# Shift and scale of x and context in two column halves with 2 KB rows, four channel chunks multiplied while the second half loads

## The chip, the cores and the metric

The kernel runs on one NeuronCore of one Trainium2 chip. The metric is the device time of one execution in microseconds; a run's time is compared as the median of several runs. The profile is of one execution of its own.

## The reference

One layer of a diffusion trunk on 512 latent tokens and 256 context tokens of width 1024. Both streams are normalised and modulated per channel by shift and scale, which are products of a conditioning vector with `w_mod`; three token mixers and a mixture of experts follow. What matters here is the start:

```python
mod_x = (sc @ w_mod[layer] + b_mod[layer]).reshape(-1, N_MOD, d)
mod_c = (scc @ w_mod[layer][:, :n_mod_c * d] + b_mod[layer][:n_mod_c * d]).reshape(1, n_mod_c, d)
hx = modulate(rms_norm(x, g_mix[layer]), mod_x[:, 0], mod_x[:, 1])
hc = modulate(rms_norm(ctx, g_mix[layer]), mod_c[:, 0], mod_c[:, 1])
px = split_columns(hx @ w_in[layer])
```

`sc` and `scc` are the silu of `c` and `c_ctx` (1024 each), `w_mod` is 1024 x 6144, and its first 2048 columns (shift, then scale) are the ones used at this place. `hx` and `hc` are multiplied with `w_in`.

## The kernel before

All is kept with channels on the 128 partitions, so the 1024 channels are eight chunks, k = 0 to 7. Products in f32 are made of two parts (a high half in fp32r and the rest as the low half): `hx` and `hc` are stored as such pairs, and every product of a weight chunk with a channel chunk is three matmuls (`quantum`, L310).

The stage this is about is `start` (L700). It computes the first two column units of `w_in`: the values (`wv`) and keys (`wk`) of the first retention head, for x (into PSUM tiles `px` and `om`, 512 columns) and for the context (into `oc`, 256 columns). Its steps per chunk k:

- `load_mod(k)` (L227) loads two tiles `wm` of 512 KB, shift and scale of chunk k: all 1024 rows of `w_mod`, 128 columns each, so rows of 512 bytes.
- `mod_rows` (L235) multiplies both tiles with the two conditioning vectors (`cpad`, 32 columns of which two are used). The eight row blocks go to four column groups of TensorE, two blocks each in turn; ScalarE copies the outcome (`rm`).
- `mod_cols` (L246) turns the outcome into columns with two small matmuls and adds the four groups; VectorE then makes `modT` and `am`.
- `turn_x`, `turn_c` (L255, L261) transpose the normalised x and context on TensorE, and `modulate` (L267) makes the high half on ScalarE and the low half on VectorE (`tf`, then the subtraction).
- `prod` (L721) makes the products of chunk k.

The order is written out by hand: from L732 to L812 `pinned` keeps the program order on every engine. The loop at L790 handles chunks 2 to 7; each round prepares chunk k + 1, makes the products of k, and makes `mod_rows` of k + 2. `pump.prime` and `pump.prime2` load and split weights of the later units, whose products (line 119) a scheduler may put between those of the stage. `tick` spreads small steps of the retention decays over the loop. `wm`, x and context share a pool of 14 tiles (L82). SyncE issues every load in order: four x tiles, wm of chunk 0, a `w_in` tile, wm of chunk 1, two context tiles, a `w_in` tile, and the other wm.

Of the kernel before, what the change touches and what calls it, by code (L numbers as in the profile page):

```python
# [8 lines left out]
F32 = mybir.dt.float32  # L9
# [40 lines left out]
def kernel(ctx, tc, x, c, cctx_x, c_ctx, w_mod, b_mod, g_mix, g_ffn, w_in, decay, ret_gn, w_ret,  # L50
# [20 lines left out]
    def dap(t, offset, ap):  # L71
        return bass.AP(tensor=t.tensor, offset=t.offset + offset, ap=ap)
# [15 lines left out]
    def h2(dtype=F32, name="h2", shape=(P, 512)):  # L88
        return H2p.tile(list(shape), dtype, name=name, tag="h2")
# [28 lines left out]
    def mm(o, lhsT, rhs, start, stop):  # L118
        PE.matmul(o, lhsT, rhs, start=start, stop=stop)  # L119
# [102 lines left out]
    def row_norm(i0, i1, half, E=V):  # L222
        for i in range(i0, i1):
            v = xs[i][:, half * 512:half * 512 + 512]
            E.tensor_scalar(v, v, rstd[:, i:i + 1], None, op0=OP.mult)

    def load_mod(k):  # L227
        ts = []
        for part in range(2):
            t = Tp.tile([P, KT, P], F32, name="wm", tag="t")  # L230
            SY.dma_start(t, dap(w_mod, part * D + k * P, [[NM, P], [P * NM, KT], [1, P]]))
            ts.append(t)
        return ts

    def mod_rows(wt):  # L235
        o = px()
        for part in range(2):
            for k2 in range(2):
                for g in range(4):
                    mm(o[32 * g:32 * g + 32, P * part:P * part + P], cpad[:, 4 * k2 + g, :],  # L240
                       wt[part][:, 4 * k2 + g, :], k2 == 0, k2 == 1)
        rm = h2(name="rm", shape=(P, 2 * P))
        A.activation(rm, o[:, 0:2 * P], AF.Copy)
        return rm

    def mod_cols(k, rm):  # L246
        o = px()
        for j in range(2):
            mm(o[:, 2 * j:2 * j + 2], rm[:, j * P:(j + 1) * P], sel2, True, True)
        b_ = colv[:, 16:32].rearrange("p (a k) -> p a k", a=2)[:, :, k:k + 1]  # L250
        V.tensor_tensor(modT[:, :, k, :], o[:, 0:4].rearrange("p (a n) -> p a n", a=2), b_.to_broadcast([P, 2, 2]),
                        op=OP.add)
        V.tensor_scalar(am[:, k, :], modT[:, 1, k, :], 1.0, colv[:, 32 + k:33 + k], op0=OP.add, op1=OP.mult)

    def turn_x(k):  # L255
        o = pa()
# [442 lines left out]

    def start():  # L700
        us = [r0[0], r0[2]]
        wm = [load_mod(0)]
        raw = [us[0].load()]
        wm.append(load_mod(1))
        for i in range(2):
            xs.append(Tp.tile([P, D], F32, name="xs", tag="t"))
            SY.dma_start(xs[4 + i], dap(cctx_x, i * P * D, [[D, P], [1, D]]))
        raw.append(us[1].load())
        wm.append(load_mod(2))
        wm.append(load_mod(3))  # L710

        def halves(raw, nm, E):
            r = []
            for b in range(2):
                hi, lo = [h2(F32R, name=nm, shape=(P, 4, P)) for _ in range(2)]
                A.activation(hi, raw[:, 4 * b:4 * b + 4, :], AF.Copy)
                E.tensor_tensor(lo, raw[:, 4 * b:4 * b + 4, :], f32(hi), op=OP.subtract)
                r.append((hi, lo))
            return r

        def prod(i, k, x=True, c=True):  # L721
            w = wsp[i][k // 4]
            us[i].quantum(k % 4, w, om[i][0] if x else None, om[i][1] if c else None, k=k)

        def mod_x(k, o):
            modulate(HX(k), HX(k, 1), o, k, 0)

        def mod_c(k, o):
            modulate(HC(k), HC(k, 1), o, k, 1)

        om = [(px(), OC()[:, :CTX]), (pa("om"), pa("oc")[:, :CTX])]
        pinned[0] = True  # L732
        for i in (0, 2):
            row_stat(i, i + 2)
            row_norm(i, i + 2, 0)
        ox, oc, rm = {}, {}, {}
        wsp = []

        dg = decays()

        def tick(n=2):
            for _ in range(n):
                next(dg, None)

        def rows_of(k):
            rm[k] = mod_rows(wm[k])
            if k < 4:
                wm.append(load_mod(k + 4))

        rows_of(0)  # L750
        ox[0] = turn_x(0)
        if HV == 0:
            wsp.append(halves(raw[0], "wv", V))
        mod_cols(0, rm[0])
        if HV == 1:
            wsp.append(halves(raw[0], "wv", V))
        mod_x(0, ox[0])
        ox[1] = turn_x(1)
        if HV == 2:
            wsp.append(halves(raw[0], "wv", V))  # L760
        rows_of(1)
        mod_cols(1, rm[1])
        prod(0, 0, c=False)
        mod_x(1, ox[1])
        wsp.append(halves(raw[1], "wk", G))
        row_stat(4, 6)
        prod(0, 1, c=False)
        row_norm(4, 6, 0)
        rows_of(2)
        prod(1, 0, c=False)  # L770
        mod_cols(2, rm[2])
        ox[2] = turn_x(2)
        prod(1, 1, c=False)
        oc[0] = turn_c(0)
        mod_c(0, oc[0])
        mod_x(2, ox[2])
        oc[1] = turn_c(1)
        mod_c(1, oc[1])
        rows_of(3)
        for i in range(2):  # L780
            prod(i, 0, x=False)
        oc[2] = turn_c(2)
        mod_c(2, oc[2])
        for i in range(2):
            prod(i, 1, x=False)
        ox[3] = turn_x(3)
        row_norm(0, 6, 1)
        rope_table(0)
        pump.prime()
        for k in range(2, KT):  # L790
            tick(T0)
            if k < 7:
                mod_cols(k + 1, rm[k + 1])
                tick(T1)
                mod_x(k + 1, ox[k + 1])
                tick(T2)
            for i in range(2):
                prod(i, k, c=False)
            if k < 7:
                oc[k + 1] = turn_c(k + 1)  # L800
                mod_c(k + 1, oc[k + 1])
                tick(T3)
            if k < 6:
                rows_of(k + 2)
            for i in range(2):
                prod(i, k, x=False)
            if k < 6:
                ox[k + 2] = turn_x(k + 2)
            if k == 5:
                pump.prime2()  # L810
        tick(99)
        pinned[0] = False  # L812
        ph0.close()
        pools["k3"] = ph1.enter_context(tc.tile_pool(name="k3p", bufs=11))
        pools["s5"] = ph1.enter_context(tc.tile_pool(name="s5p", bufs=8))
        for u, o in zip(us, om):
            u.done(*o)
# [906 lines left out]
```

## Time and profile before

| what | value |
|---|---|
| median of 3 runs | 1224.18 us (1221.31 to 1225.31) |
| the profiled execution | 1222.83 us |
| its span, first to last instruction | 1221.1 us |
| TensorE matmuls busy (PE) | 1156.3 us (95%) |
| TensorE weight loads (PEld) | 720.6 us (59%) |
| VectorE (DVE) | 618.3 us (51%) |
| ScalarE (ACT) | 402.9 us (33%) |
| GpSimd (POOL) | 87.7 us (7%) |
| mean DMA rate | 234 GB/s over 285.57 MB |

Times in rows are microseconds from the start of the span. PE is TensorE, and a matmul of f32 operands shows as two instructions. A busy engine is not the same as an engine at its peak: matmuls are pipelined, so of a row of equal matmuls the distance between starts is the price, not the duration of one. "Idle before <- X" says what ended an engine's wait.

### The profile page before, as it was taken

The page shows a single profiled execution, that of the slowest core. Times are in us where ns is not written, and L with a number is a line of the kernel's source. Part 1 is how long each engine was busy: PE and PEld are TensorE (multiplying, and loading weights), DVE is VectorE, ACT ScalarE, POOL GpSimd, SP SyncE. Part 2 cuts the span into 40 slices and gives each one's busy share as a digit, 9 for nine tenths or more (in the row PEclk, how much of TensorE's full clock was granted, in tenths as well). Part 3 has the DMA queues.
Part 4 walks back from the last instruction along what each step waited for, and adds up shares of the span by engine and source line. Part 5 has one row for each costly group of instructions (what it writes and reads, how often), then busy time and mean ns, then how long its engine had stood idle before and what let it go on. Part 6 is the DMA issues. An engine that isn't in the chain of part 4 may idle for free.

```text
span 1221.1 us, 15830 instructions
## 1 busy us (share of the span) xinstructions
PE 1156.3 (95%) x5869; PEld 720.6 (59%) x5869; DVE 618.3 (51%) x1383; ACT 402.9 (33%) x777; POOL 87.7 (7%) x149
## 2 busy tenths in 40 slices
PE   4999999899999999999999969999999999999995
PEld 2788888777668887788888854333333323233322
DVE  3787666788867764577646362233332222222213
ACT  4553334666645553333332222122111111111112
POOL 2011111100041120000000000000000000000001
PEclk9999999999999999999999979999999999999998
DMA  9822112211012115987638548999999999999994
GB/s 272 232 75 70 52 52 89 57 38 34 12 52 61 42 54 198 285 268 248 199 95 300 194 161 298 409 409 409 409 409 409 409 409 409 409 409 408 409 409 188
DMA packets 159978, 285.57 MB, mean 234 GB/s; under 512 B 10838, under 2 KB 100250, under 8 KB 159900
## 3 DMA queue, kind: packets, MB, share of 16 engines
q1 hardware_dynamic: 158172, 278.27, 62.7%
q0 software_dynamic: 1152, 4.19, 0.9%
q10 hardware_dynamic: 576, 2.10, 0.4%
q8 instruction: 46, 0.75, 0.3%
q14 instruction: 32, 0.26, 0.1%
HBM read 280.33 MB, written 4.19 MB: 233 GB/s over the span
## 4 chain that ended last, share of the span: by engine, by line
PE 61%; DMA 25%; DVE 8%; ACT 2%; issue 1%; SPq 1%; POOL 1%; DVEq 0%; POOLq 0%; ACTq 0%
PE px L119 26%; DMA rg<-in_w_exp_up_dram 16%; PE pa L67 10%; PE px L67 8%; DMA rg<-in_w_exp_down_dram 7%; PE pa L119 7%; PE PV L119 3%; PE oc L119 3%; DVE ws L295 1%; PE pa L1041 1%; PE pa L955 1%; PE oy L119 1%; DMA rw<-in_w_in_dram 1%; DMA wm<-in_w_mod_dram 1%; DVE rt L445 1%
## 5 line engine op out<-in xcount | busy, mean ns | idle before, releaser
L67 PE MATMUL pa<-rg,xe 128*64 128x512 f32 x1024 | 263.3, 607 | 7.1 <-DMA rg<-in_w_exp_up_dram 4.8
L67 PEld LDWEIGHTS pa<-rg,xe 128*64 128x64 f32 x1024 | 72.5, 137 | 154.8 <-issue 108.2
L67 PE MATMUL px<-rg,hid 128*64 128x512 f32 x512 | 120.3, 601 | 10.7 <-DMA rg<-in_w_exp_down_dram 9.9
L295 DVE TENSOR_TENSOR ws<-rw,ws 128x1024 fp32r<-128x1024 f32 x55 | 67.7, 1232 | 56.1 <-PE px L119 34.7
L67 PEld LDWEIGHTS px<-rg,hid 128*64 128x64 f32 x512 | 32.8, 136 | 90.2 <-issue 48.2
L119 PE MATMUL px<-hx0h,ws 128*128 128x512 f32 x224 | 83.3, 401 | 0.0
L119 PE MATMUL px<-hx3h,ws 128*128 128x512 f32 x224 | 83.3, 398 | 0.0
L119 PE MATMUL px<-hx1h,ws 128*128 128x512 f32 x224 | 82.6, 398 | 0.0
L119 PE MATMUL px<-hx2h,ws 128*128 128x512 f32 x224 | 82.2, 395 | 0.0
L67 DVE SCALAR_TENSOR_TENSOR tt<-px,gcol,m 128x512 f32<-128x512 f32 x16 | 12.0, 751 | 127.6 <-PE px L67 127.6
L67 ACT ACTIVATE yy<-tt 64x512 fp32r<-64x512 f32 x32 | 20.1, 628 | 144.6 <-DVE tt L67 144.2
L67 DVE TENSOR_TENSOR acc<-px,acc 128x512 f32<-128x512 f32 x58 | 37.5, 687 | 59.9 <-PE px L67 59.9
L119 PE MATMUL px<-yh,ws 128*128 128x512 f32 x192 | 62.3, 390 | 0.6 <-ACT mod L1165 0.6
L294 ACT ACTIVATE ws<-rw 128x1024 fp32r<-128x1024 f32 x55 | 57.8, 1052 | 5.6 <-DMA rw<-in_w_in_dram 5.1
L911 ACT ACTIVATE Sx<-Sx,nm 128x512 f32<-128x512 f32 (+1 forms) x64 | 47.9, 748 | 34.4 <-DVE nm L947 19.0
L1160 DVE SCALAR_TENSOR_TENSOR mac<-mw,cpad,mac 128x1024 f32<-128x1024 f32 x30 | 38.5, 1282 | 17.9 <-DMA mw<-in_w_mod_dram 15.6
L119 PEld LDWEIGHTS px<-hx3h,ws 128*128 128x128 f32 x224 | 42.1, 189 | 7.9 <-issue 1.1
L119 PEld LDWEIGHTS px<-hx0h,ws 128*128 128x128 f32 x224 | 42.2, 189 | 7.6 <-issue 0.7
L119 PEld LDWEIGHTS px<-hx1h,ws 128*128 128x128 f32 x224 | 42.3, 189 | 7.2
L119 PEld LDWEIGHTS px<-hx2h,ws 128*128 128x128 f32 x224 | 42.4, 189 | 6.9
L67 ACT ACTIVATE gu<-pa 128x512 f32<-128x512 f32 x16 | 9.5, 596 | 110.0 <-PE pa L67 110.0
L67 DVE TENSOR_SCALAR xe<-px,af,sf 128x128 f32<-128x128 f32 (+1 forms) x36 | 14.0, 403 | 62.1 <-ACT xe L67 43.3
(422 smaller groups left out, 2169.6 us busy)
## 6 DMA issues: line engine op xcount, KB each, us to landing
rg<-in_w_exp_gate_dram SPq DMA_DIRECT2D x128, 512.0 KB, 10.2
rg<-in_w_exp_up_dram SPq DMA_DIRECT2D x128, 512.0 KB, 10.2
rg<-in_w_exp_down_dram SPq DMA_DIRECT2D x128, 512.0 KB, 10.2
rw<-in_w_in_dram SPq DMA_DIRECT2D x58, 512.0 KB, 4.0
mw<-in_w_mod_dram SPq DMA_DIRECT2D x32, 512.0 KB, 5.2
wm<-in_w_mod_dram SPq DMA_DIRECT2D x16, 512.0 KB, 7.7
rw<-in_w_out_dram SPq DMA_DIRECT2D x8, 512.0 KB, 3.6
xs<-in_x_dram SPq DMA_DIRECT2D x4, 512.0 KB, 4.1
```

The lines of the kernel that those rows point to most:

```text
L67: return (lambda *a_, **k_: tc.keep_in_program_order(f(*a_, **k_))) if pinned[0] else f
L119: PE.matmul(o, lhsT, rhs, start=start, stop=stop)
L294: A.activation(hi, raw, AF.Copy)
L295: V.tensor_tensor(lo[:, :NV], raw[:, :NV], f32(hi[:, :NV]), op=OP.subtract)
L445: V.tensor_copy(t2[b:b + q], o[c:c + q])
L911: A.activation(Sx[:, :n], Sx[:, :n], AF.Exp, scale=-1.0, bias=nm, accum_out=l[:, 0:1])
L955: PE.transpose(o[:, j * P:(j + 1) * P], SXs[b, j][:, ti * P:(ti + 1) * P], ident)
L1041: PE.transpose(o[:, b * P:(b + 1) * P], SXs[a, b][:, ti * P:(ti + 1) * P], ident)
L1160: V.scalar_tensor_tensor(macs[w], tiles[i], cpad[:, k, 0:1], macs[w], op0=OP.mult, op1=OP.add)
```

## The change

The first 2048 columns of `w_mod` are loaded and multiplied in two halves: half 0 has shift and scale of chunks 0 to 3, half 1 those of chunks 4 to 7. A tile is two row blocks by 512 columns, so its rows are 2 KB. `load_mod(half, kp)` loads two such tiles (shift, scale), and `mod_rows` makes four matmuls of 512 columns per pair `kp`, into two PSUM tiles that collect the four pairs of a half. `mod_cols` runs once per half: two copies, eight small matmuls, and three VectorE instructions for four chunks. All of half 0 is loaded and multiplied ahead of the first product. In a loop over k = 0 to 3 the products of chunk k stand beside `mod_rows` of pair k of half 1; then `mod_cols` of half 1 and a loop over k = 4 to 7. The context products of both units share the PSUM tile `oc`. The normalising of the second halves of x and context moves into rounds 0 and 1.

```diff
-    def load_mod(k):
+    def load_mod(half, kp):
...
         for part in range(2):
-            t = Tp.tile([P, KT, P], F32, name="wm", tag="t")
-            SY.dma_start(t, dap(w_mod, part * D + k * P, [[NM, P], [P * NM, KT], [1, P]]))
+            t = Tp.tile([P, 2, 512], F32, name="wm", tag="t")
+            SY.dma_start(t, dap(w_mod, 2 * kp * P * NM + part * D + half * 512, [[NM, P], [P * NM, 2], [1, 512]]))
             ts.append(t)
...
-    def mod_rows(wt):
-        o = px()
+    def mod_rows(mo, kp, ts):
         for part in range(2):
-            for k2 in range(2):
-                for g in range(4):
-                    mm(o[32 * g:32 * g + 32, P * part:P * part + P], cpad[:, 4 * k2 + g, :],
-                       wt[part][:, 4 * k2 + g, :], k2 == 0, k2 == 1)
...
+            for i in range(2):
+                k = 2 * kp + i
+                g = k % 4
+                mm(mo[part][32 * g:32 * g + 32, :], cpad[:, k, :], ts[part][:, i, :], k < 4, k >= 4)
...
+    def mod_cols(half, mo):
+
+        o = pa("mc")
+        for part in range(2):
+            rm = h2(name="rm")
+            if part:
+                V.tensor_copy(rm, mo[part])
+            else:
+                A.activation(rm, mo[part], AF.Copy)
+            for j in range(4):
+                c_ = 8 * part + 2 * j
+                mm(o[:, c_:c_ + 2], rm[:, j * P:(j + 1) * P], sel2, True, True)
...
+        raw, wm = [us[0].load()], {}
+        for kp in range(4):
+            wm[0, kp] = load_mod(0, kp)
...
+        wsp = [halves(raw[0], "wv", V)]
+        ox, oc = {}, {}
+        mo = [px(), px()]
+        for kp in range(4):
+            mod_rows(mo, kp, wm[0, kp])
+            wm[1, kp] = load_mod(1, kp)
         ox[0] = turn_x(0)
...
+        mod_cols(0, mo)
+        row_stat(4, 6)
         mod_x(0, ox[0])
         ox[1] = turn_x(1)
...
         row_norm(4, 6, 0)
...
+        mo = [px(), px()]
+        for k in range(4):
+            prod(0, k, c=False)
+            if k == 0:
+                wsp.append(halves(raw[1], "wk", G))
+            oc[k] = turn_c(k)
+            mod_c(k, oc[k])
+            if k < 3:
+                mod_x(k + 1, ox[k + 1])
+                if k < 2:
+                    ox[k + 2] = turn_x(k + 2)
+            prod(1, k, c=False)
+            mod_rows(mo, k, wm[1, k])
+            for i in range(2):
+                prod(i, k, x=False)
+            if k == 0:
+                row_norm(0, 4, 1)
+            if k == 1:
+                row_norm(4, 6, 1)
+            tick(6)
         rope_table(0)
         pump.prime()
...
+        ox[4] = turn_x(4)
+        mod_cols(1, mo)
+        mod_x(4, ox[4])
+        ox[5] = turn_x(5)
+        oc[4] = turn_c(4)
+        mod_c(4, oc[4])
+        for k in range(4, KT):
             if k < 7:
...
                 mod_x(k + 1, ox[k + 1])
...
             for i in range(2):
                 prod(i, k, c=False)
```

The order of the loads on SyncE's queue, before, from the last x tile on (`xs` are x and context tiles, `rw` tiles of `w_in`):

```order
L148 DMA xs<-in_x_dram 128x1024
L150 DMA sink_b<-in_win_sink_dram 128x8
L231 DMA wm<-in_w_mod_dram 128x8x128 x2
L289 DMA rw<-in_w_in_dram 128x8x128
L231 DMA wm<-in_w_mod_dram 128x8x128 x2
L707 DMA xs<-in_ctx_dram 128x1024 x2
L289 DMA rw<-in_w_in_dram 128x8x128
L231 DMA wm<-in_w_mod_dram 128x8x128 x12
```

The same place in the changed kernel:

```order
L148 DMA xs<-in_x_dram 128x1024
L150 DMA sink_b<-in_win_sink_dram 128x8
L298 DMA rw<-in_w_in_dram 128x8x128
L232 DMA wm<-in_w_mod_dram 128x2x512 x8
L716 DMA xs<-in_ctx_dram 128x1024 x2
L298 DMA rw<-in_w_in_dram 128x8x128
L232 DMA wm<-in_w_mod_dram 128x2x512 x8
```

The context and the second `w_in` tile move behind eight wm tiles instead of four, and the first `w_in` tile ahead of them.

TensorE's order at the beginning of the stage, before (a row of wm is `mod_rows`, of rm `mod_cols`, of xs transposes):

```order
L67 MATMUL px<-wm,cpad 32x128 x16
L67 MATMUL pa<-cs,xs 128x128 x4
L67 MATMUL px<-cs,rm 128x2 x2
L67 MATMUL pa<-cs,xs 128x128 x4
L67 MATMUL px<-wm,cpad 32x128 x16
L67 MATMUL px<-cs,rm 128x2 x2
L67 MATMUL px<-hx0h,wv 128x512
L67 MATMUL px<-hx0l,wv 128x512
```

And in the changed kernel:

```order
L67 MATMUL px<-wm,cpad 32x512 x16
L67 MATMUL pa<-cs,xs 128x128 x4
L67 MATMUL mc<-cs,rm 128x2 x8
L67 MATMUL pa<-cs,xs 128x128 x4
L67 MATMUL px<-hx0h,wv 128x512
L67 MATMUL px<-hx0l,wv 128x512
L67 MATMUL px<-hx0h,wv 128x512
L67 MATMUL pa<-cs,xs 128x128 x6
L67 MATMUL om<-hx0h,wk 128x512
L67 MATMUL om<-hx0l,wk 128x512
L67 MATMUL om<-hx0h,wk 128x512
L67 MATMUL px<-wm,cpad 32x512 x4
```

Sixteen products of 512 columns stand ahead of the first wv product where sixteen of 128 columns, and a second such set, stood; the second half's follow four at a time between the products of chunks 0 to 3.

VectorE's order behind the first `mod_cols` in the changed kernel (`rs_v`, `rs_t`, `rstd` are the context's reciprocal root, which before stood behind the low half of chunk 1):

```order
L67 COPY rm<-px 128x512
L67 TENSOR_TENSOR modT<-mc,colv 128x8 x2
L67 SCALAR_TENSOR_TENSOR am<-modT,colv 128x8
L67 TENSOR_SCALAR rs_v<-ssq 128x2
L67 TENSOR_TENSOR rs_t<-rstd 128x2
L67 TENSOR_TENSOR rs_t<-rs_t,rs_v 128x2
L67 TENSOR_SCALAR rs_t<-rs_t 128x2
L67 TENSOR_TENSOR rstd<-rstd,rs_t 128x2
L67 TENSOR_SCALAR tf<-pa,am,modT 128x512
L67 TENSOR_TENSOR hx0l<-tf,hx0h 128x512
L67 TENSOR_SCALAR xs<-xs,rstd 128x512 x2
```

The root moved ahead of `tf` and the low half of chunk 0.

## Rows read from the trace of the kernel before

**Rows 1.** Windows: length, busy us (count) by engine, clock, DMA share, GB/s.

```profile
14.00:31.60 17.60, 14.68 (x121) 9.60 (x122) 8.35 (x23) 7.09 (x13) 4.60 (x5) 1.00 1.14 308
...
43.20:59.70 16.50, 16.47 (x185) 14.18 (x186) 12.57 (x41) 9.61 (x17) 0.43 (x1) 1.00 0.72 188
...
80.00:200.00 120.00, 118.91 (x598) 97.42 (x597) 86.95 (x156) 47.18 (x69) 23.03 (x22) 1.00 0.24 71
```

**Rows 2.** Waits of TensorE, 12 to 62 us: total, times, longest.

```profile
PE px L67 <- DMA wm<-in_w_mod_dram: 5.4, 4, 4.0
```

**Rows 3.** Timeline of ScalarE: start, us, instruction, idle before and what ended it.

```profile
12.21 1.06 ACT L67 ACTIVATE junk<-xs 128x1024 f32<-128x1024 f32 x1 [1.66 <-DMA xs<-in_x_dram]
```

**Rows 4.** Timeline of TensorE, early in the stage.

```profile
17.79 0.85 PE L67 MATMUL px<-cs,rm 128*128 128x2 f32 x4
...
29.20 1.08 PE L67 MATMUL px<-wm,cpad 128*32 128x128 f32 x16 [0.29 <-DMA wm<-in_w_mod_dram]
```

**Rows 5.** Windows with 512 byte rows, then with 4 KB rows.

```profile
24.00:30.00 6.00, 4.94 (x38) 2.43 (x37) 2.09 (x5) 4.01 (x7) 3.62 (x4) 1.00 1.17 290
...
654.00:656.00 2.00, 2.00 (x14) 1.73 (x13) 1.60 (x2) 0.78 (x2) 0.00 (x0) 1.00 1.02 414
```

**Rows 6.** Timeline of TensorE, first and last unit product ahead of the stage's end.

```profile
59.70 0.40 PE L119 MATMUL px<-hx0h,ws 128*128 128x512 f32 x1
...
64.02 0.39 PE L119 MATMUL px<-hx3h,ws 128*128 128x512 f32 x1
...
66.09 0.60 PE L484 MATMUL pa<-cs,vt 128*128 128x128 f32 x4
```

**Rows 7.** The page's DMA issues: count, KB each, us to landing.

```profile
rw<-in_w_in_dram SPq DMA_DIRECT2D x58, 512.0 KB, 4.0
...
rw<-in_w_out_dram SPq DMA_DIRECT2D x8, 512.0 KB, 3.6
```

**Rows 8.** Timeline of TensorE, one channel step.

```profile
43.69 0.51 PE L67 MATMUL px<-cs,rm 128*128 128x2 f32 x4
44.06 0.48 PE L67 MATMUL px<-hx1h,wv 128*128 128x512 f32 x1
...
45.53 0.38 PE L67 MATMUL pa<-cs,xs 128*128 128x128 f32 x2
45.84 1.08 PE L67 MATMUL px<-wm,cpad 128*32 128x128 f32 x32
46.86 0.39 PE L67 MATMUL oc<-hc0h,wv 128*128 128x256 f32 x1
...
47.67 0.60 PE L67 MATMUL pa<-cs,xs 128*128 128x128 f32 x4
48.11 0.51 PE L67 MATMUL px<-cs,rm 128*128 128x2 f32 x4
```

**Rows 9.** Timeline of TensorE, gate and up products of the experts.

```profile
733.44 3.68 PE L67 MATMUL pa<-rg,xe 128*64 128x512 f32 x8
...
741.59 1.94 PE L67 MATMUL pa<-rg,xe 128*64 128x512 f32 x8
```

**Rows 10.** The page's groups: out<-in xcount, busy, mean ns, idle before.

```profile
L67 ACT ACTIVATE gu<-pa 128x512 f32<-128x512 f32 x16 | 9.5, 596 | 110.0 <-PE pa L67 110.0
```

**Rows 11.** Timeline of VectorE, early in the stage.

```profile
20.83 0.81 DVE L67 TENSOR_SCALAR tf<-pa,am,modT 128x512 f32<-128x512 f32 x1 [0.91 <-ACT hx0h L67]
21.67 0.69 DVE L67 TENSOR_TENSOR hx0l<-tf,hx0h 128x512 fp32r<-128x512 f32 x1
...
24.02 0.23 DVE L67 TENSOR_SCALAR am<-modT,colv 128x2 f32<-128x2 f32 x1
...
28.83 0.20 DVE L67 TENSOR_SCALAR rs_v<-ssq 128x2 f32<-128x2 f32 x1 [2.20 <-ACT junk L67]
...
30.90 0.88 DVE L67 TENSOR_SCALAR xs<-xs,rstd 128x512 f32<-128x512 f32 x2
```

**Rows 12.** Window with the gate products of 733 us.

```profile
732.00:736.00 4.00, 4.00 (x14) 2.19 (x15) 0.71 (x6) 1.21 (x5) 1.22 (x1) 0.50 0.10 11
```

More of the change, by code (lines that the diff above doesn't have):

```diff
@@ L232, in load_mod @@
             ts.append(t)
         return ts
-    def mod_rows(wt):
-        o = px()
+    def mod_rows(mo, kp, ts):
         for part in range(2):
-            for k2 in range(2):
-                for g in range(4):
-                    mm(o[32 * g:32 * g + 32, P * part:P * part + P], cpad[:, 4 * k2 + g, :],
-                       wt[part][:, 4 * k2 + g, :], k2 == 0, k2 == 1)
[L242 to L253, printed above, removed]
+            for i in range(2):
+                k = 2 * kp + i
+                g = k % 4
+                mm(mo[part][32 * g:32 * g + 32, :], cpad[:, k, :], ts[part][:, i, :], k < 4, k >= 4)
@@ new lines, in mod_cols @@
+    def mod_cols(half, mo):
[9 more added lines that the diff above has]
+                mm(o[:, c_:c_ + 2], rm[:, j * P:(j + 1) * P], sel2, True, True)
+        ks = slice(4 * half, 4 * half + 4)
+        for part in range(2):
+            b_ = colv[:, 16 + 8 * part + 4 * half:20 + 8 * part + 4 * half]
+            V.tensor_tensor(modT[:, part, ks, :], o[:, 8 * part:8 * part + 8].rearrange("p (k n) -> p k n", n=2),
+                            b_[:, :, None].to_broadcast([P, 4, 2]), op=OP.add)
+        gm = colv[:, 32 + 4 * half:36 + 4 * half]
+        V.scalar_tensor_tensor(am[:, ks, :], modT[:, 1, ks, :], 1.0, gm[:, :, None].to_broadcast([P, 4, 2]),
+                               op0=OP.add, op1=OP.mult)
@@ L701, in start @@
         us = [r0[0], r0[2]]
-        wm = [load_mod(0)]
-        raw = [us[0].load()]
-        wm.append(load_mod(1))
+        raw, wm = [us[0].load()], {}
+        for kp in range(4):
+            wm[0, kp] = load_mod(0, kp)
         for i in range(2):
@@ L708, in start @@
         raw.append(us[1].load())
-        wm.append(load_mod(2))
-        wm.append(load_mod(3))
         def halves(raw, nm, E):
@@ L719, in halves @@
             return r
+        occ = OC()
+        om = [(px(), occ[:, :CTX]), (pa("om"), occ[:, CTX:])]
         def prod(i, k, x=True, c=True):
-            w = wsp[i][k // 4]
-            us[i].quantum(k % 4, w, om[i][0] if x else None, om[i][1] if c else None, k=k)
+            hi, lo = wsp[i][k // 4]
+            j, f, l = k % 4, k == 0, k == KT - 1
+            if x:
+                o = om[i][0]
+                mm(o, hi[:, j, :], HX(k), f, False)
+                mm(o, hi[:, j, :], HX(k, 1), False, False)
+                mm(o, lo[:, j, :], HX(k), False, l)
+            if c:
+                o = om[i][1]
+                mm(o, hi[:, j, :], HC(k), f and i == 0, False)
+                mm(o, hi[:, j, :], HC(k, 1), False, False)
+                mm(o, lo[:, j, :], HC(k), False, l and i == 1)
         def mod_x(k, o):
@@ L729, in mod_c @@
             modulate(HC(k), HC(k, 1), o, k, 1)
-        om = [(px(), OC()[:, :CTX]), (pa("om"), pa("oc")[:, :CTX])]
         pinned[0] = True
[L733 to L737, printed above, removed]
         dg = decays()
@@ L743, in tick @@
                 next(dg, None)
[L745 to L750, printed above, removed]
-        ox[0] = turn_x(0)
[L752 to L756, printed above, removed]
+        for i in (0, 2):
+            row_stat(i, i + 2)
+            row_norm(i, i + 2, 0)
+        wsp = [halves(raw[0], "wv", V)]
@@ L757, in start @@
+        ox, oc = {}, {}
[3 more added lines that the diff above has]
+            wm[1, kp] = load_mod(1, kp)
+        ox[0] = turn_x(0)
+        mod_cols(0, mo)
+        row_stat(4, 6)
         mod_x(0, ox[0])
         ox[1] = turn_x(1)
[L759 to L765, printed above, removed]
@@ L766, in start @@
-        row_stat(4, 6)
-        prod(0, 1, c=False)
-        row_norm(4, 6, 0)
[L769 to L785, printed above, removed]
@@ L786, in start @@
-        ox[3] = turn_x(3)
-        row_norm(0, 6, 1)
+        row_norm(4, 6, 0)
+        mo = [px(), px()]
[18 more added lines that the diff above has]
+            tick(6)
@@ L788, in start @@
         rope_table(0)
         pump.prime()
-        for k in range(2, KT):
-            tick(T0)
+        ox[4] = turn_x(4)
[5 more added lines that the diff above has]
+        for k in range(4, KT):
             if k < 7:
-                mod_cols(k + 1, rm[k + 1])
-                tick(T1)
                 mod_x(k + 1, ox[k + 1])
-                tick(T2)
             for i in range(2):
@@ L801, in start @@
                 mod_c(k + 1, oc[k + 1])
-                tick(T3)
-            if k < 6:
-                rows_of(k + 2)
             for i in range(2):
@@ L810, in start @@
                 pump.prime2()
+            tick(4)
         tick(99)
```

## The prediction

> **What bounds the kernel now.** I read the windows first. The kernel's opening stage, from the first weight tile to the last product of the stage at 66.1 us, falls into two halves [rows 1]: from 14.0 to 31.6 us TensorE is busy 14.68 of 17.6 us while the DMA engines are full (308 GB/s); from 43.2 to 59.7 it is busy 16.47 of 16.5 us while the DMA share falls. So the stage begins on transfers and ends on TensorE. Behind it, TensorE is busy 118.9 of 120 us [rows 1], so what the stage gains or loses is handed on to the end almost whole.
>
> Then the waits of TensorE in the stage: on shift and scale tiles (`wm`) it loses 5.4 us in four waits, and 4.0 of these are the first one [rows 2]. That is all that faster tiles can give back while TensorE keeps its order of work.
>
> Then the transfers. The last x tile is used at 12.21 us [rows 3], and the second tile of the third shift and scale load at 29.20 us [rows 4]. Ten transfers of 512 KB land in between (six wm, two w_in, two context): 17.0 us, 1.70 us each. With long rows the same engines move 414 GB/s against 290 here [rows 5], which is 1.27 us for 512 KB.
>
> **Bound of the stage's end before.** The last product is issued just ahead of 66.09 us. Between 59.70 and 64.02 us stand 19 products of the next units (line 119), which belong to later work [rows 6]. The 6.39 us up to 66.09 hold these 19, six x products and 0.8 us of context products, so one takes 5.6 / 25 = 0.22 us; without the 19 the stage would end at 66.1 - 4.2 = 61.9 us. The change is to be held against that.
>
> **The change part by part.**
>
> *First tiles.* All of the first half (4 MB) must now land before the first product; before, 1 MB was enough. The queue is x, one w_in load, then eight tiles. After 12.2 us: w_in 1.7, giving 13.9; eight tiles with 2 KB rows. No row shows a run of 2 KB rows; the bounds are 1.27 us (4 KB rows) and 1.70 us (512 byte rows). Alone, a 2 KB load lands after 3.6 us and a 512 byte one after 4.0 [rows 7], a difference of 0.4, so I take 1.3: 13.9 + 10.4 = **24.3 us** (27.5 at the other end). The Trainium skill, DMA: Bandwidth & Descriptors, section Specifications, calls 512 B the smallest transfer for line rate; by that rule the tiles would stay at 1.7 us and the sum would be 3.2 us longer. The 290 against 414 GB/s speak against the rule.
>
> *Products of shift and scale.* Before, eight chunks stood in four column groups in turn and a channel's 16 products took 1.02 us (45.84 to 46.86) [rows 8]. Now a pair of tiles has four products of 512 columns that use two groups only. The nearest row with two groups is gate and up: the same eight instructions of 512 columns take 1.94 us, and 3.68 us when the clock is at its low level [rows 9]; I take 1.9. In the first half only the last tile's two products remain after its landing: 0.9, giving **25.2 us**, if the earlier pairs kept up with a pair each 2.6 us. At the low level they do not: 4 x 3.7 from 15.2 us ends at 29.9.
>
> *Column products.* Now eight in one go behind a copy of 512 columns on ScalarE (0.6 us [rows 10]) and one on VectorE beside it; with the hand-over 26.0 us. Two took 0.37 us at the high level (43.69 to 44.06) [rows 8]; eight take 1.5, or 3.0 at the low level that the row at 17.79 shows (0.85 against 0.51 for four instructions) [rows 4, 8]. TensorE does little between 25 and 29 us, so I take 2.2: 28.2. Then two `modT` and one `am` on VectorE, about 0.25 each with their hand-overs [rows 11], 1.0 in all: **29.2 us**.
>
> *VectorE's queue.* The context's reciprocal root now stands between `am` and channel 0's low half: from `rs_v` to the normalising of xs 2.07 us (28.83 to 30.90) [rows 11], most of it a wait for GpSimd. The context has landed by then (24.3 + 2 x 1.3 = 26.9) and its squares are through by 29. So `tf` starts at 31.2, and with 0.84 and 0.69 [rows 11] the low half is there at **32.7 us**. ScalarE's high half lies under that. The context's first transposes wait for the normalising behind it: 0.4 us more on TensorE.
>
> *TensorE's work from there*, at the prices of one channel step before [rows 8]: x products 1.47, a context transpose 0.31, shift and scale 1.02, context products 0.81, x transpose 0.44, column products 0.37. Channels 0 and 1 now: 1.47 + 0.65 + 1.9 + 0.81 = 4.83 each; channels 2 and 3, without x transposes, 4.49; together 18.6. In the middle 0.44 + 1.5 + 0.65 = 2.6. Channels 4 to 7: 4 x 2.28 + 3 x 0.31 + 2 x 0.44 = 10.9. Sum 32.1, less one product done early: 31.9. That is not less than before: the second half costs 4 x 1.9 where the last four channels before cost 4 x 1.02, which is 3.5 us more, and it is here on the path. The second half's tiles land by 24.3 + 2.6 + 1.7 + 10.4 = 39.0 us while TensorE wants the last near 47: these transfers are hidden and their speed is worth nothing.
>
> *A hole in the middle.* Channel 4's halves can't be made before the second half's columns are there, and after channel 3 nothing else stands in TensorE's order. Behind the column products: 1.0 (modT, am) + 0.78 (high half) less the 0.65 of transposes, then 0.81 + 0.69 for the low half [rows 11] less one product: about 2.4 us. Before, each channel was modulated a step ahead of its products.
>
> *Clock.* The granted clock column says 1.00 throughout the stage, yet the row at 17.79 us takes 0.85 us where the one at 43.69 takes 0.51: the early rows run at the 1.2 GHz level, the later ones at 2.4. In the later stretch whose column says 0.50, the gate row takes 3.68 us against 1.94 [rows 9, 12]. The change leaves TensorE with little between 25 and 33 us, so channel 0 likely begins at the low level. Bounds: nothing, or a whole channel step at half speed (+4.8); I take the middle, 2.4.
>
> The sum: 32.7 + 31.9 + 0.4 + 2.4 + 2.4 = 69.8 us, against 61.9: **7.9 us later**. The profiled execution took 1222.83 us (span 1221.1 and 1.7 around it), so 1230.7; the median of the runs, 1224.18, lies 1.35 higher. I say **1231 us**. Decay steps, masks and the later units keep their order and lie under TensorE's work: nothing.
>
> **Rivals.**
> - *Transfers stay the bound (faster).* If four channels' work fits under the second half's loading, the stage ends at 39.0 + 0.9 (last products) + 4.1 (copy 0.8, columns 1.5, modT and am 1.0, high half 0.8) + 1.3 (low half) + 10.9 = 56.2 us: 5.7 us earlier, 1217. It decides if TensorE has done 18.6 us of work by 40, so if the first product starts by 21. For it: the full DMA engines in the first stretch and the 5.4 us of waits [rows 1, 2]. Against it: the first half alone lands at 24.3, and [rows 1] show TensorE as the later bound. 0.06.
> - *About no change.* The two column groups run as well as four (4 x 0.9 back), the clock is high at channel 0 (2.4 back) and the column products take 1.5 (0.7 back): 7.9 - 6.7 = 1.2 us, 1224. Against it the gate row with two groups at 1.94 us [rows 9]. 0.16.
> - *Low clock through the first half.* Products end at 29.9 instead of 25.2: 7.9 + 4.7 = 12.6, 1235. Before, the level was low until past 18 us although such products ran. 0.15.
> - *2 KB rows are no faster:* 27.5 instead of 24.3: 7.9 + 3.2, 1234. The change then does not do what its first part says. 0.08.
>
> **How the numbers follow.** The forecast, 4 to 11 us later, has 0.55. A measurement here tells about 0.3% (3.7 us) from no change. Faster by more: 0.06, the first rival. Within it: the second rival and a little of the forecast's lower end, 0.19. Slower: 0.75. The range leaves out the first rival and the tail in which several costs meet: 1223 to 1237.
>
> **What the profile should show.** Right: the first wv product on hx0 near 30 us and the last product of channel 7, without those of later units, near 70; wm landing every 1.3 us; eight wm instructions in about 1.9 us; a hole of 2 to 3 us ahead of channel 4; no wait on wm in the second half. Wrong: wm waits inside the channel loop (transfers bound after all), 1 us for the eight wm instructions, or a first product before 25 us.

## The result and the profile after

The changed kernel takes 1230.82 us (median of 4 runs, 1229.69 to 1231.81) against 1223.93 us before (4 runs, 1221.31 to 1225.31): a ratio of 1.0052, 95% interval 1.0037 to 1.0068. It is slower by over 0.3%, and within 0.2 us of the forecast of 1231. The profiled execution took 1229.69 us with a span of 1227.9 (before: 1222.83 and 1221.1).

The windows of the changed kernel, the first two and the last as in [rows 1]: length, busy us (count) of PE, PEld, DVE, ACT and POOL, then clock, DMA share and GB/s.

```profile
14.00:31.60 17.60, 12.80 (x57) 4.42 (x57) 4.88 (x15) 5.86 (x10) 1.53 (x2) 1.00 1.05 380
...
43.20:59.70 16.50, 14.85 (x86) 8.91 (x83) 10.24 (x35) 5.94 (x11) 0.00 (x0) 0.98 0.21 45
80.00:200.00 120.00, 119.19 (x598) 97.75 (x597) 88.04 (x157) 47.36 (x69) 21.43 (x21) 1.00 0.23 67
```

The transfers became faster (380 GB/s where 308 stood) and TensorE nevertheless did less: 12.80 us busy instead of 14.68 in the opening, 14.85 instead of 16.47 in the middle, where the DMA engines have almost nothing to move. From 80 to 200 us the two kernels are alike (119.19 and 118.91 us busy).

Where TensorE waits, 12 to 75 us, to hold against [rows 2]: total, times, longest.

```profile
PE px L67 <- DVE wv L67: 5.9, 1, 5.9
PE px L67 <- DVE hx0l L67: 3.1, 1, 3.1
PE px L67 <- DVE hx2l L67: 1.1, 1, 1.1
PE px L67 <- ACT hx0h L67: 0.9, 1, 0.9
PE px L67 <- DMA wm<-in_w_mod_dram: 0.9, 3, 0.3
PE px L67 <- ACT hx2h L67: 0.6, 1, 0.6
```

The first line is the start, ahead of any product; the first tile lands there too (the `w_in` tile ahead of it was used at 14.64 us, and a tile takes 1.36). Before, the start was 4.0 of the 5.4 us put down to tiles [rows 2], so without it the waits on tiles went from 1.4 to 0.9 us, all of them in the first half. What is new are waits on halves of `hx`: 3.1 + 0.9 us ahead of channel 0, and 1.1 + 0.6 ahead of channel 4 (`hx2h` and `hx2l` hold channels 4 and 5).

TensorE's timeline of the changed kernel, from the first tile to the stage's end (what [rows 4], [rows 6] and [rows 8] showed of before):

```profile
22.79 1.05 PE L67 MATMUL px<-wm,cpad 128*32 128x512 f32 x4 [0.29 <-DMA wm<-in_w_mod_dram]
...
25.50 1.05 PE L67 MATMUL px<-wm,cpad 128*32 128x512 f32 x4 [0.30 <-DMA wm<-in_w_mod_dram]
...
26.97 1.84 PE L67 MATMUL mc<-cs,rm 128*128 128x2 f32 x16
...
33.87 0.80 PE L67 MATMUL px<-hx0l,wv 128*128 128x512 f32 x1 [3.14 <-DVE hx0l L67]
34.46 0.63 PE L67 MATMUL px<-hx0h,wv 128*128 128x512 f32 x1
...
40.66 0.40 PE L67 MATMUL px<-hx0h,wv 128*128 128x512 f32 x1
40.89 0.40 PE L67 MATMUL px<-hx0l,wv 128*128 128x512 f32 x1
...
42.81 1.91 PE L67 MATMUL px<-wm,cpad 128*32 128x512 f32 x8
44.65 0.39 PE L67 MATMUL oc<-hc0h,wv 128*128 128x256 f32 x1
...
45.47 0.39 PE L67 MATMUL px<-hx1h,wv 128*128 128x512 f32 x1
...
57.87 0.49 PE L67 MATMUL px<-hx2h,wv 128*128 128x512 f32 x1 [0.57 <-ACT hx2h L67]
59.44 0.79 PE L67 MATMUL px<-hx2l,wv 128*128 128x512 f32 x1 [1.08 <-DVE hx2l L67]
60.03 0.63 PE L67 MATMUL px<-hx2h,wv 128*128 128x512 f32 x1
60.46 0.63 PE L67 MATMUL om<-hx2h,wk 128*128 128x512 f32 x1
...
73.20 0.60 PE L493 MATMUL pa<-cs,vt 128*128 128x128 f32 x4
```

A tile is used every 1.36 us, the last of the half at 25.50, and the second wv product starts only at 33.87. Channel 1 (40.66 to 45.47) takes 4.81 us, of which the pair of tiles takes 1.84 (42.81 to 44.65). A hole stands ahead of channel 4, and the place that stood at 66.09 [rows 6] is now at 73.20. Eleven products of line 119 stand between instead of 19, at 0.23 us each, so the stage itself ends at 73.20 - 2.5 = 70.7 us, against 61.8 by the same working: 8.9 us later. "End of the stage" below means this number throughout. What follows the products of 34.46 and 60.03 starts 0.43 us behind them; behind the one of 40.66 it is 0.23.

The clock in shorter windows of the same stage, columns as above:

```profile
30.00:34.00 4.00, 0.64 (x2) 0.32 (x2) 3.62 (x7) 1.21 (x3) 3.44 (x4) 0.71 1.05 387
31.00:32.00 1.00, 0.00 (x0) 0.00 (x0) 1.00 (x2) 0.21 (x1) 1.00 (x2) 0.82 1.06 393
34.00:38.00 4.00, 4.00 (x13) 2.72 (x15) 1.92 (x4) 1.69 (x3) 0.10 (x1) 0.50 1.05 388
...
58.00:62.00 4.00, 2.92 (x8) 2.02 (x9) 3.10 (x5) 1.39 (x3) 0.00 (x0) 0.62 0.00 0
59.50:62.00 2.50, 2.50 (x7) 1.91 (x8) 1.63 (x3) 0.00 (x0) 0.00 (x0) 0.50 0.00 0
```

The granted clock falls to 0.50 (1.2 GHz) twice. The first time it falls between 31 and 32 us, inside the wait for channel 0's low half, and stays low over channel 0's products. The second time it falls in the hole, behind the small column products, and stays low over the first products of channel 4.

### The profile page after: what moved, and what is told of

Read it like the earlier page. It is cut to its first block, busy times and chain, and to the rows that moved or that the text cites. A ratio compares the mean times of both kernels' runs of the same rounds, so it can differ in the third digit from the quotient of the medians.

```text
span 1227.9 us, 15416 instructions
## 1 busy us (share of the span) xinstructions
PE 1160.4 (94%) x5677; PEld 714.6 (58%) x5677; DVE 619.0 (50%) x1375; ACT 401.3 (33%) x771; POOL 86.5 (7%) x149
## 4 chain that ended last, share of the span: by engine, by line
PE 66%; DMA 23%; DVE 7%; ACT 1%; issue 1%; POOL 1%; SPq 0%; DVEq 0%; POOLq 0%; ACTq 0%
PE px L119 27%; DMA rg<-in_w_exp_up_dram 14%; PE pa L67 11%; PE px L67 9%; PE pa L119 7%; DMA rg<-in_w_exp_down_dram 7%; PE PV L119 3%; PE oc L119 3%; PE pa L1047 1%; PE pa L961 1%; PE oy L119 1%; DVE ws L304 1%; DMA wm<-in_w_mod_dram 1%; DVE rt L454 1%; PE oc L67 1%
```

## The experiments

All are edits of the changed kernel. Since the moment at which the tiles land shifts by about a microsecond from one execution to the next, the table also has the distance from the last tile of half 0 (first use) to the end of the stage. The quarters' last eleven context products stand behind the place where the stage's end is read (74.08 to 75.49 us); their 1.4 us are counted in.

| kernel | ratio to before, 95% interval | end of stage, us | last tile used | distance |
|---|---|---|---|---|
| before | 1 | 61.8 | | |
| the change | 1.0052 [1.0037, 1.0068] | 70.7 | 25.50 | 45.2 |
| four groups | 1.0032 [1.0016, 1.0048] | 68.8 | 25.59 | 43.2 |
| early columns | 1.0021 [1.0009, 1.0034] | 66.1 | 25.49 | 40.6 |
| root on GpSimd | 1.0062 [1.0040, 1.0083] | 71.0 | 24.84 | 46.2 |
| fillers | 1.0040 [1.0019, 1.0061] | 69.7 | 25.79 | 43.9 |
| 512 B rows | 1.0076 [1.0054, 1.0099] | 74.1 | | |
| 512 B rows, half 1 | 1.0068 [1.0043, 1.0092] | 70.8 | 25.06 | 45.7 |
| wk on VectorE | 1.0049 [1.0030, 1.0068] | 70.0 | 25.15 | 44.8 |
| early, four, wk | 1.0008 [0.9997, 1.0020] | 62.9 | 24.57 | 38.3 |
| the same and root | 1.0006 [0.9994, 1.0018] | 63.4 | 25.02 | 38.3 |
| the same and fillers | 1.0009 [0.9997, 1.0020] | 64.2 | 25.28 | 38.9 |
| quarters | 1.0041 [1.0027, 1.0055] | 69.5 | 20.54 | 49.0 |

In the times, only the early columns and the three rows that contain them are clear of the change; the other intervals overlap with its own. The stage is read from one profile each, and the stretches of low clock in it differ between kernels that do the same there. From channel 0's second product to channel 1's first, the change takes 6.79 us, and early columns, wk on VectorE and short rows in half 1 take 6.13 to 6.23. From channel 4's second product to channel 5's first, the kernels that keep the hole take 3.88 to 4.71 us. So a difference of under a microsecond in the distance isn't settled by one profile; where it matters, the rows themselves are read below.

**Four column groups.** A pair of row blocks uses groups 0 and 1 or 2 and 3, for shift and scale alike. Here scale takes the two that shift leaves free.

```diff
-                g = k % 4
+                g = (k + 2 * part) % 4
```

> The four products of a pair of wm tiles use four column groups instead of two (scale is put two groups further than shift). My account: the eight wm instructions fall from 1.84 us to about 1.0 us, four times on the path in the channel loop, so the stage ends 3.3 us earlier than in the changed kernel (70.7 to 67.4) and the run takes 1227 to 1228 us. Rival, two groups run at the same pace as four because the moving operand sets the pace: 1.84 us stays and the run stays at 1231.

The pair fell from 1.84 to 1.0 us, and the end of the stage came 1.9 us earlier, not 3.3. TensorE's timeline of this kernel shows where the rest stayed:

```profile
41.41 1.06 PE L67 MATMUL px<-wm,cpad 128*32 128x512 f32 x8
...
44.36 0.50 PE L67 MATMUL px<-hx1l,wv 128*128 128x512 f32 x1 [0.69 <-DVE hx1l L67]
45.94 1.07 PE L67 MATMUL px<-wm,cpad 128*32 128x512 f32 x8
...
48.67 0.50 PE L67 MATMUL px<-hx1l,wv 128*128 128x512 f32 x1 [0.53 <-DVE hx1l L67]
```

Two new waits of 0.69 and 0.53 us on the low halves of channels 2 and 3 came up: the pairs had covered VectorE's work. So the two groups are a real cost, of which a third was cover for another engine.

**Early columns.** The second half's tiles are multiplied in rounds 0 (pair 0), 1 (pairs 1 and 2) and 2 (pair 3), and its column products stand ahead of round 3, whose products then cover channel 4's modulation.

```diff
-            if k < 3:
+            if k < 4:
                 mod_x(k + 1, ox[k + 1])
...
-            mod_rows(mo, k, wm[1, k])
+            for kp in ((0,), (1, 2), (3,), ())[k]:
+                mod_rows(mo, kp, wm[1, kp])
             for i in range(2):
                 prod(i, k, x=False)
+            if k == 2:
+                ox[4] = turn_x(4)
+                mod_cols(1, mo)
...
-        ox[4] = turn_x(4)
-        mod_cols(1, mo)
-        mod_x(4, ox[4])
```

> The second half's products move up (pair 0 in round 0, pairs 1 and 2 in round 1, pair 3 in round 2), the column products follow in round 2 and chunk 4 is modulated in round 3 before its products. My account: the hole ahead of channel 4 (1.65 us of idle TensorE) goes, and with it the half speed behind it (granted clock 0.50 from 59.5 to 62.0 us, worth about 1.2 us): 2.5 to 3 us earlier, 1228. No wait on wm comes up, since the last tile is there by 40 us. Rival, the second half's loading is not hidden: waits on wm of 2 us and more in rounds 1 and 2, and no gain.

The stage ended 4.6 us earlier, more than expected. Both waits on `hx2` are gone, and with them the second fall of the clock. The windows of this kernel at the place of the hole:

```profile
54.00:58.00 4.00, 3.89 (x25) 3.31 (x26) 3.42 (x11) 2.38 (x5) 0.00 (x0) 1.00 0.00 0
58.00:62.00 4.00, 3.94 (x26) 3.32 (x26) 3.41 (x10) 2.72 (x6) 0.00 (x0) 1.00 0.01 4
```

And the two pairs that now stand in a row take together what one took, from TensorE's timeline of this kernel:

```profile
37.34 1.91 PE L67 MATMUL px<-wm,cpad 128*32 128x512 f32 x8
42.13 1.94 PE L67 MATMUL px<-wm,cpad 128*32 128x512 f32 x16
46.53 1.91 PE L67 MATMUL px<-wm,cpad 128*32 128x512 f32 x8
```

Pair 1 uses groups 2 and 3, pair 2 groups 0 and 1: side by side they overlap. The 4.6 us are then, by this account, 1.65 (the hole), 1.2 (the clock behind it) and 1.8 (a pair for nothing); the last was not expected.

**The context's root on GpSimd.**

```diff
-        row_stat(4, 6)
+        row_stat(4, 6, G)
```

> The context's reciprocal root is computed on GpSimd alone, so VectorE goes from am straight to tf of chunk 0. My account: hx0l is there about 2.3 us earlier than at 33.87 us (it then waits for ScalarE's high half, 30.1, and takes 0.8 and 0.7), the first context transposes at most 0.5 us later, so 1.5 to 2 us earlier in all, 1229. Rival, the stage is bound by the first half's landing and TensorE's work alone, and the order on VectorE is worth nothing: the second wv product starts earlier, but the context's transposes wait as long as before and the run stays at 1231.

A miss. The second wv product did come 2.7 us earlier, at 31.16, but the stage ended no earlier. VectorE's row of the context's scaling, in this kernel:

```profile
31.20 2.88 DVE L67 TENSOR_SCALAR xs<-xs,rstd 128x512 f32<-128x512 f32 x2
```

GpSimd's row beside it:

```profile
31.12 2.68 POOL L67 TENSOR_TENSOR wk<-rw,wk 128x512 fp32r<-128x512 f32 x2
```

Two scalings take 0.88 us alone [rows 11], and 2.88 here, to within 0.3 us of the end of GpSimd's subtraction. The context's transposes waited for them instead (0.35 and 0.93 us), and the low clock lasted longer over channel 0: the pair of tiles behind its products took 3.29 us where the change has 2.33.

**wk on VectorE.** So GpSimd's subtraction was taken away from there.

```diff
-                wsp.append(halves(raw[1], "wk", G))
+                wsp.append(halves(raw[1], "wk", V))
```

> The low half of the keys' weights is made on VectorE, behind the context's normalising, instead of on GpSimd; nothing else. My new account of the low half of chunk 0: GpSimd's subtraction (30.8 to 33.3 us) slows what VectorE does beside it (rstd took 1.21 us instead of 0.16, hx0l 1.00 instead of 0.69). Without it rstd takes 0.2 and hx0l 0.7, so hx0l is ready 1.3 us earlier (second wv product at 32.5 instead of 33.87) and the stage ends 1 to 1.5 us earlier, 1229.5 to 1230. Rival, rstd waits there for something else (its own operands): it keeps 1.2 us and the VectorE work added makes the stage 1 us longer.

First the rows of VectorE in the changed kernel, while GpSimd's two `wk` instructions run from 30.77 to 33.26 us:

```profile
30.84 1.21 DVE L67 TENSOR_TENSOR rstd<-rstd,rs_t 128x2 f32<-128x2 f32 x1
31.98 0.80 DVE L67 TENSOR_SCALAR tf<-pa,am,modT 128x512 f32<-128x512 f32 x1
32.81 1.00 DVE L67 TENSOR_TENSOR hx0l<-tf,hx0h 128x512 fp32r<-128x512 f32 x1
```

Then the same two instructions with GpSimd idle:

```profile
30.81 0.16 DVE L67 TENSOR_TENSOR rstd<-rstd,rs_t 128x2 f32<-128x2 f32 x1
31.73 0.69 DVE L67 TENSOR_TENSOR hx0l<-tf,hx0h 128x512 fp32r<-128x512 f32 x1
```

An instruction on 128 x 2 elements took 1.21 us instead of 0.16, and ended when the first of GpSimd's two would have (30.77 + 1.24); `tf`, which reads PSUM, kept its 0.80. The second wv product came at 32.47, 1.4 us earlier, and channel 4's second product at 57.48 instead of 59.44, 1.96 earlier (0.35 of that is the earlier landing). The stage gained only 0.4 to 0.7, where 1 to 1.5 were expected, because the clock stayed low longer behind the hole: from that product to channel 5's first it took 4.71 us instead of 3.88. The windows of this kernel there:

```profile
58.00:62.00 4.00, 4.00 (x16) 3.43 (x15) 1.68 (x4) 1.02 (x2) 0.00 (x0) 0.50 0.00 0
62.00:66.00 4.00, 4.00 (x24) 3.53 (x23) 2.35 (x6) 2.27 (x4) 0.00 (x0) 0.86 0.02 4
```

Why it stayed low longer is not shown. No new wait of TensorE came up where VectorE now splits `wk`.

The Trainium skill, SBUF — State Buffer, section Who interferes with whom, says that a VectorE instruction with two SBUF inputs contends with a GpSimd instruction that reads SBUF, that one in a two-port mode contends with GpSimd too, and that whichever issues second waits for the other to finish. The rows agree for `rstd` (two SBUF inputs), which waited, and for `tf` with its PSUM input, which did not; `hx0l`, 0.3 us longer, waited in part. `xs` has one SBUF input and waited; whether it ran in a two-port mode no run shows.

**Fillers.** Useless products of wv with itself keep TensorE busy: 22 ahead of channel 0's second product (8 of them ahead of the first). Their results are thrown away.

```diff
+        filler(8)
         for k in range(4):
...
                 mm(o, hi[:, j, :], HX(k), f, False)
+                if i == 0 and k == 0:
+                    filler(14)
```

> 22 products of 512 columns without use (a wv chunk with wv weights, into a PSUM tile that is overwritten later) fill TensorE's idle time from 28.9 to 33.9 us, 8 ahead of the first wv product and 14 behind it. My account: the granted clock stays at its high level there, and the products of channel 0 take 0.40 us instead of 0.63 from the start: half of the 4.6 us at 0.50, 2.3 us earlier, 1228.5. Rival, the low level is no matter of the idle time before it (or channel 0 is held by its operands anyway): no gain, or the fillers' own time is added, 1231 to 1234.

The windows of this kernel:

```profile
30.00:34.00 4.00, 4.00 (x20) 3.29 (x19) 3.29 (x6) 1.51 (x3) 3.47 (x4) 1.00 1.04 386
34.00:38.00 4.00, 4.00 (x23) 2.28 (x21) 2.25 (x5) 1.69 (x3) 0.44 (x1) 1.00 1.04 386
58.00:62.00 4.00, 3.85 (x15) 3.36 (x16) 2.20 (x6) 1.13 (x3) 0.00 (x0) 0.60 0.02 4
```

Channel 0 ran at the high level: from its second product to channel 1's first it took 4.56 us instead of 6.79. The rows of the loop came 1.3 to 1.4 us earlier, not 2.3, since the fillers themselves ran about 0.5 us past the low half. The fall in the middle stayed. The low clock at channel 0 is thus a cost of its own.

**Rows of 512 bytes, in both halves and in the second alone.** The same columns, each tile by two loads of 256 KB (one per row block) of 128 partitions x 4 pieces x 128 columns, and the pieces land apart in the tile. So four pieces of 512 bytes stand where a row of 2 KB stood, though they still lie side by side in `w_mod`. The products are the same.

```diff
-            SY.dma_start(t, dap(w_mod, 2 * kp * P * NM + part * D + half * 512, [[NM, P], [P * NM, 2], [1, 512]]))
+            for i in range(2):
+                SY.dma_start(t[i], dap(w_mod, off + i * P * NM, [[NM, P], [P, 4], [1, P]]))
```

> Both halves are loaded with rows of 512 bytes (each tile by two loads of 256 KB, one per row block), all else as in the changed kernel. My account: a tile takes 1.7 us instead of 1.36, so the last tile of the first half is there 2.7 us later (25.5 to 28.2) and the stage ends 2.5 to 3 us later; the run takes 1233.5. Rival, TensorE's own work on the first half sets its end (it is busy 9.0 of 12 us from 14 to 26): less than 1 us later.

> Only the second half is loaded with rows of 512 bytes; the first half keeps 2 KB. My account: the second half is hidden, its last tile is there near 43 us and used at 51.5: no wait on wm, the stage's end and the run as in the changed kernel, 1231. Rival, the second half's speed counts: 2 us and more later, with waits on wm in the rounds.

Where both halves have short rows, the first half's products end at 29.4 us, 2.85 later, and the stage 3.4 later. The first half in the changed kernel, then in this one:

```profile
14.00:26.00 12.00, 8.99 (x32) 1.64 (x32) 2.39 (x6) 1.75 (x3) 0.00 (x0) 1.00 1.04 390
14.00:26.00 12.00, 11.05 (x25) 1.96 (x26) 2.73 (x8) 1.06 (x2) 0.12 (x1) 1.00 1.17 290
```

It is 290 GB/s against 390. The smaller loads are not the reason: the kernel before moved 290 GB/s too, with rows of 512 bytes in loads of 512 KB [rows 5]. So the change does what its first part says. Where only the second half has short rows, the end of the stage is the same (70.8), no pair in the rounds waits for `wm`, and the rows up to channel 4 are no later than in the change (57.87 there, 56.77 here). The time's interval overlaps with the change's. (One row names `wm`, 2.84 us ahead of channel 0's second product, but that product waits there for its low half, and 2.8 to 3.1 us of wait stand at the same place with long rows.) The second half's transfers are hidden, at either speed.

The Trainium skill, DMA: Bandwidth & Descriptors, section Specifications, has line rate from 512 bytes on; the 2.85 us and the 290 against 390 GB/s contradict it for these loads.

**Three edits together:** early columns, four groups, wk on VectorE.

> Three undoings together: the second half's products in rounds 0 to 2 with its columns ahead of round 3, the two pairs of a half on different column groups, and the low half of wk on VectorE. If the parts of the excess are separate, the end of the stage (70.7 us in the changed kernel, 66.1 with the early products alone) comes to 66.1 less 1.6 for two pairs of four groups instead of two, less 0.7 to 1.4 for the undisturbed VectorE: 63 to 64, still 1 to 2 behind the kernel before (61.8), and the time to 1225 to 1226. The rival: TensorE is not what bounds the rounds any more, and what it saves it waits for operands of VectorE and ScalarE, as it did in part with four groups alone: end of the stage at 65 to 66, time 1227.

**The same with the root on GpSimd, and the same with fillers (8 and 10).**

> As the kernel with the three undoings, with the context's root on GpSimd, which has no tile of wk to split now. If the root failed before only because it met GpSimd's wk, the second wv product comes near 31.2 us, the context's scaling takes 0.9 instead of 2.9, and the stage ends 1 to 1.5 earlier than without it (62 to 63, time 1224 to 1225, the kernel before's). The rival: wk's split on VectorE stands ahead of the scaling instead, the context's transposes wait as long, and nothing is gained.

> As the kernel with the three undoings, with 8 useless products ahead of the first wv product and 10 behind it (their result is thrown away). If the low clock of channel 0 is still a cost of its own there, it is worth what it was in the changed kernel (1.0 to 1.4 of stage): end of the stage 62 to 63, time about 1225. The rival: with the second wv product earlier, the fillers stand in its way and the gain is under 0.5.

The distance shrinks by 6.9 us, and alone the edits gave 4.6, 2.0 and 0.4. The sum fits, though not part by part: with early columns only two of the four pairs are left for four groups to shorten, and there is no hole behind which the gain of wk could be lost. The stage's end, 62.9, is a little ahead of the 63 to 64 expected. The ratio is 1.0008 [0.9997, 1.0020]: of the loss, no part is left that is clear of the noise (1.1 us in the stage by this one profile), and nothing is won. TensorE's waits in this kernel, 12 to 75 us (5.0 of the first line are the start):

```profile
PE px L67 <- DMA wm<-in_w_mod_dram: 6.3, 5, 5.0
PE px L67 <- DVE hx0l L67: 1.8, 1, 1.8
PE px L67 <- ACT hx0h L67: 0.9, 1, 0.9
PE oc L67 <- DVE hc0l L67: 0.5, 1, 0.5
```

The root on GpSimd and the fillers brought nothing more, as both rivals said, though the first not for its reason: the context's scaling stood ahead of wk's split and took 1.47 us. With the root moved, `hx0l` was waited for 0.85 us instead of 1.76, but the products of channel 0 then ran longer at the low level (clock 0.66 instead of 0.83 between 34 and 38 us) and the pair met it too. With fillers channel 0 ran at the high level, but the low halves of channels 2 and 5 came late (0.33 and 0.26 us of wait) and the clock fell later instead, to a mean of 0.67 between 50 and 54 us.

Not tried: the first `w_in` tile behind the tiles of half 0. The change put it ahead of them, and the first tile was used at 16.11 us, where before it was at 14.19.

**Quarters.** Four steps of 256 columns (rows of 1 KB), two channels each, four groups; a quarter's products stand between those of the quarter ahead of it; wk on VectorE, the root on GpSimd.

```diff
-            t = Tp.tile([P, 2, 512], F32, name="wm", tag="t")
+            t = Tp.tile([P, 4, 256], F32, name="wm", tag="t")
```

> Four quarters of 256 columns (1 KB rows, two channels each) in place of two halves, on four column groups, the products of a quarter standing between those of the quarter ahead of it, the low half of wk on VectorE and the context's root on GpSimd. If the excess came only from waiting for a whole half and from the second half's products in pairs on two groups, then the first quarter is there after some 18.6 us instead of 25.5 (five loads of 1.3 to 1.5 us behind x), the first wv product starts at 23, and TensorE's work behind it is 8 x 1.47 + 8 x 0.31 + 6 x 0.44 + 8 x 0.81 + 3 x 1.06 + 3 x 0.5 = 28 us plus 2.4 for the low clock: end of the stage at 54 to 57 against 61.8 before, and a time of 1217 to 1220, faster than both kernels. The rival: the operands of VectorE and ScalarE or the landing of the quarters set each step then, and what TensorE saves it waits: end of the stage near 61, time 1223 to 1225.

A miss: the rival came, and worse than it was priced. The first quarter was there at 20.5 us and the second wv product at 27.17, 6.7 us earlier than in the change, but the stage ended at 69.5. TensorE's timeline of this kernel:

```profile
43.19 1.93 PE L67 MATMUL mo<-wm,cpad 128*32 128x256 f32 x32
...
48.61 1.05 PE L67 MATMUL mc<-cs,rm 128*128 128x2 f32 x8 [1.51 <-ACT rm L67]
...
64.87 0.50 PE L67 MATMUL px<-hx3l,wv 128*128 128x512 f32 x1 [1.06 <-DVE hx3l L67]
```

The 16 products of a quarter take 1.9 us, not the 1.06 of the expectation, which had counted half of them: four groups save nothing against before, where two channels took 2 x 1.02 [rows 8]. And the copy `rm` stood behind the context's four activations on ScalarE (46.15 to 47.95 us in the second round), so its column products waited, and the modulation behind them. The order was too simple; a better one was not tried, so whether quarters can beat the kernel before stays open.

## Why the prediction was right

Step by step, predicted and measured in the profile of the changed kernel:

| step | predicted | measured |
|---|---|---|
| tiles of 512 KB | 1.3 us each | 1.36 |
| last tile of half 0 | 24.3 | 25.50 |
| end of its products | 25.2 | 26.5 |
| column products through | 28.2 | 28.8 |
| `am` | 29.2 | 29.3 |
| `tf` starts | 31.2 | 31.98 |
| low half of channel 0 | 32.7 | 33.8 |
| pair of tiles, second half | 1.9 | 1.84 |
| channel 1 | 4.83 | 4.81 |
| low clock at channel 0 | 2.4 | 2.2 |
| hole ahead of channel 4 | 2.4 | 1.65 |
| low clock behind the hole | none | 1.2 |
| end of the stage, later than before | 7.9 | 8.9 |
| time, later than before | 7.9 | 6.9 [4.5, 8.3] |

(Low clock at channel 0: 33.87 to 40.66 is 6.79 us, against 4.81 for channel 1's same work less 0.23 for the product done ahead. Low clock behind the hole: the last five x products of channel 4 take 2.30 us, 59.44 to 61.74, and channel 5's 1.15, 63.64 to 64.79.)

**The main steps held.** Transfers became faster and TensorE's wait for its first product did not become shorter, because all of a half had to land before it. TensorE set the pace of the rounds, and the second half's tiles were hidden (no wait on `wm` in any round, and none with slow rows either). The two-group price of the gate row was right for pairs; four groups took the pair to 1.0 us.

**Sizes that were off.** The term "13.9 + 10.4 = 24.3 us": the w_in tile was used at 14.64 us instead of 13.9, and eight tiles at 1.36 instead of 1.3 add 0.5. Column products cost 1.84 us and their hand-overs less than taken; that was made up by the step "the root takes 2.07 us on VectorE": it took 2.71 (29.27 to 31.98), because GpSimd's `wk` held up `rstd` by 1.05 us. The prediction had counted that root's wait for GpSimd, but not that GpSimd's next work stops VectorE. The hole was over-priced by 0.75 us, and the fall of the clock behind it, of which nothing was said, cost 1.2. These offset each other to within a microsecond. In the prices, "1.47 + 0.65 + 1.9 + 0.81" takes 0.65 for the two transposes that it lists at 0.31 and 0.44; they measured 0.58 (41.36 to 41.94). Last, the sum was put on the profiled execution (1222.83 + 7.9); on the median of 1224.18, with which a run is compared, it gives 1232.1. That the median came out within 0.2 us of 1231 is luck.

**The extra transposes' 0.4 us** did not show: TensorE went from wv's products straight to the transposes at 34.89.

**Handing on.** The prediction has what the stage loses "handed on to the end almost whole". The 8.9 us of the stage did not reach it whole: the spans differ by 6.8. Here the forecast was helped, since its stage was 1.0 us too short. The router's products start 8.1 us later (716.38 against 708.31), the last output products 6.8 (1215.38 against 1208.58). So about 1 us is given back ahead of the experts and about 1 in them; in which wait was not settled, and single executions of one kernel differ by more (1221.31 to 1225.31 us before).

**The rivals.** "Transfers stay the bound" fell on the rounds without `wm` waits. "About no change" fell on its first condition, 1.84 us for a pair. "Low clock through the first half" fell: the first half's last tiles each took about 1.0 us for two products, the high level, and products ended at 26.5. Why is open: before, such products kept to half pace until past 30 us (16 instructions in 1.02 us from 29.20 [rows 4], where 32 take as long from 45.84 [rows 8]). "2 KB rows are no faster" fell on 390 against 290 GB/s.

## What to carry to other kernels

Longer rows pay only for what waits on transfers: here 2 KB rows saved 2.85 us in the first half and nothing in the second, while the coarser step put the first two products 6.6 and 9.7 us later (23.64 and 24.21 us before, 30.23 and 33.87 now) and cost a hole where the steps meet, with the clock behind it. When a step is made coarser, put the next step's preparation ahead of the last products that could cover it (here 2.9 of the 4.6 us that the early columns gave). Column groups are worth using by instructions that stand next to each other, whatever tiles they belong to.

## What the runs showed of the hardware that was not expected

- VectorE waits for GpSimd: `rstd` 1.21 us instead of 0.16, two scalings 2.88 instead of 0.88, while GpSimd subtracts two SBUF tiles.
- Products on different column groups overlap across pairs: 16 instructions on four groups in 1.94 us, 8 on two groups in 1.91.
- The granted clock can stand at 1.00 while rows run at half pace: with quarters, the products between 28.90 and 32.46 us follow at 0.43 us under a column of 1.00, as the early rows before did [rows 4]. The distance between the starts of equal products is the safer reading; 0.43 against 0.23 us for 512 columns tells the level.
- Keeping TensorE busy at one place did not keep the clock up at the next: with fillers at channel 0 the clock still fell in the middle (mean 0.60 from 58 to 62 us), and with fillers and early columns it fell near 50 us, where without them it had stayed at 1.00. One profile each shows it; the reason is not shown.
- A stretch of low clock need not last as long in two kernels that do the same there: 3.88 and 4.71 us behind the hole, in the change and with wk on VectorE.
